# Seven products for eight in the down projection of a decoder trunk's two feed-forward blocks

## The chip, the cores and the metric

One core of a Trainium2 chip runs the whole program. TensorE (PE) multiplies, VectorE (DVE), ScalarE (ACT) and GpSimd (POOL) work on the operands and results, SyncE (SP) issues most DMAs. The metric is the device time of one execution in microseconds (us), the median of several runs.

## The reference

One layer of a hybrid decoder over 1032 tokens (1024 of a prompt, 8 decoded ones), in float32. Its frame is two half-step feed-forward blocks around a mixing block:

```python
def swiglu(x, wg, wu, wd):
    return (jax.nn.silu(x @ wg) * (x @ wu)) @ wd

h = x + 0.5 * swiglu(rmsnorm(x), wg1, wu1, wd1)     # FFN 1
u = rmsnorm(h); z = u @ w_in                        # mixing: attention and mLSTM heads
...
h = h + 0.5 * swiglu(rmsnorm(h), wg2, wu2, wd2)     # FFN 2
h = h + sigmoid(rmsnorm(h) @ w_ple_gate) * ple
```

D_MODEL is 1024, D_FF 2816. The change is in the last product of `swiglu`, the "down" product of 1032 tokens x 2816 by 2816 x 1024, which both FFNs have.

## The kernel before

Activations lie with features on the 128 partitions and tokens along the free axis. Tokens are cut in three groups of N = 344 (`GS`) or four quarters of QN = 258 (`QS`); two quarters are a half (`hf`). D_FF is NF = 22 blocks of 128 features, in NP = 11 pairs. A float32 product is made of three matmuls on operands that are split in an upper part (made by ACT, `hh`, `wh`) and a lower part (made by DVE, `hl`, `wl`); `split` writes both and `mm3` issues upper x upper, upper weight x lower activation, lower weight x upper activation, in this order. So the second matmul of a tile needs the lower part of the activation.

`ffn` does one FFN. Its **gate and up stage** already makes seven products for eight: `chain(i)` multiplies 2 x 2 blocks of weights by sums of 2 x 2 blocks of activations, on 258 tokens at a time, and leaves in the tile `hp` (128 x 4 x 258, per half of the tokens) the product of gate and up for one pair of feature blocks and two quarters. `store` writes it to device memory (`hidd`, a DMA on POOL's queue).

The **down stage** runs in five passes over (half `mh` of the 1024 outputs, group of tokens): `[(0,(0,1)),(0,(2,)),(1,(0,)),(1,(1,)),(1,(2,))]`. A pass has 22 steps, one for each feature block, and a step four blocks of 128 outputs, so that a pass holds 4 (in the first pass 8) of the eight PSUM banks. Weights (`load_wd`, 512 KB for two steps) and `hp` (`load_hid`, 516 KB for three steps) come five steps (`AHEAD_D`) ahead, each through `split`. After a pass the accumulators `pd` are added to the residual `h` on DVE (line 585: h = 0.5 * pd + h; an eviction below), and after the passes of the second output half the norm of that group for the next stage is begun (`nxt.a`: squares on ACT, sums on POOL and DVE; `nxt.b` some microseconds later: a matmul `ns` with ones, lines 276 and 242 to 244, and the multiplies `xf` of line 287).

PE and SP run in the order of the code. The order of ACT, DVE and POOL is set when the program is built, by a scheduler; on the chip each engine then runs its list in this order, and an instruction that waits holds up those behind it.

Of the kernel before, what the change touches and what calls it, by code (L numbers as in the profile page):

```python
# [7 lines left out]
F32 = mybir.dt.float32  # L8
F32R = mybir.dt.float32r
# [6 lines left out]
D = 1024  # L16
# [3 lines left out]
G = 3  # L20
# [7 lines left out]
HC = 2 * QN  # L28
NPAIR = NF // 2
NCH = 2 * NPAIR  # L30
AHEAD_D = 5
HEADS = 8
MH = 4
CH = 128
# [9 lines left out]
POOL_LO = 5  # L44
NBIG = 43
LAT_B = 5.0
LAT_IN = (5.0, 4.0, 12.0)
LAT_P = (5.0, 5.0, 20.0)
AH_IN = {(3, 12): (0,), (4, 4): (1,), (4, 12): (2,)}
PL_A, PL_B = 13, 5  # L50
BUILD_AT = (2, 4, 5, 6)
AH_P = {(3, 12): (0,), (4, 4): (1,), (4, 10): (2,), (4, 16): (3,)}
POOL_FIN = (1, 3, 5)
FIN_ORDER = (0, 1, 2, 4, 3, 6, 5, 7)
PJ = 2
# [84 lines left out]
def trunk(ctx: ExitStack, tc, I, O):  # L140
# [249 lines left out]
    def ffn(build, X, pre, part, resid, h, nxt, ahead, lat, aheads):  # L390

        W = [I["wg" + part], I["wu" + part]]
        wd = I["wd" + part]
        hidd = tc.dram_tile([NF, 128, T], F32, name="hid" + part)
        wraw, ops, gens = pre

        def want(i):
# [22 lines left out]

        gs = [None, None]

        def store(i, hf, o):
            pool.dma_start(out=hidd[i - 1:i + 1, :, hf * HC:(hf + 1) * HC].rearrange("a p c -> p a c"),  # L426
                           in_=o.rearrange("p (a q) n -> p a (q n)", a=2))

        def plain(i, hf):
            o = B([128, 4, QN], F32, "hp" if i % 2 else "gs")  # L430
            for q in range(2):
                for a in range(2):
                    ps = PS([128, QN], "cp")
                    for kh in range(2):
                        mm(ps, ops[i]["p%d" % (2 * a + kh)], X[hf][("b1", "b2")[kh] + "12"[q]], kh == 0, kh == 1)
                    d = o[:, 2 * a + q]
                    if i % 2 == 0:
                        act.activation(d, ps, AF.Silu)
                    else:
                        dve.tensor_tensor(out=d, in0=ps, in1=gs[hf][:, 2 * a + q], op=ALU.mult)  # L440
                yield
            if i % 2 == 0:
                gs[hf] = o
            else:
                gs[hf] = None
                X[hf].pop("b12")
                store(i, hf, o)
            if hf == 1:
                ops.pop(i)

        def chain(i):
# [4 lines left out]
            def product(ps, n, first, lst):  # L456
                for hf in range(2):
                    mm(ps[hf], ops[i][n], X[hf][n], first, lst)
                    yield hf
                ops[i].pop(n)  # L460
                if last:
                    for hf in range(2):
                        X[hf].pop(n)
                    fetch(("b11", "b21", "t2", "t1", "t3", "t4").index(n) - 1 if n != "b22" else AHEAD_D)

            for hf in range(2):
                b1[hf] = PS([128, QN], "c1")
# [34 lines left out]
            for hf in product(b3, "b22", False, True):  # L502
                dve.tensor_tensor(out=o[hf][:, 1], in0=b3[hf], in1=u2[hf], op=ALU.add)
                b3[hf] = u2[hf] = None
                if not up:
                    act.activation(o[hf][:, 1], o[hf][:, 1], AF.Silu)
                    gs[hf] = o[hf]
                else:
                    for a, b in ((0, 2), (3, 4)):
                        dve.tensor_tensor(out=o[hf][:, a:b], in0=o[hf][:, a:b], in1=gs[hf][:, a:b], op=ALU.mult)  # L510
                    gs[hf] = None
                    store(i, hf, o[hf])
                o[hf] = None
            ops.pop(i)
            ready(i + 1)
            want(i + 2)


        passes = [(0, (0, 1)), (0, (2,)), (1, (0,)), (1, (1,)), (1, (2,))]
        seq = [(p, f) for p in range(len(passes)) for f in range(NF)]  # L520
        wdh, hid = {}, {}

        def load_wd(mh, p):
            raw = B([128, 2, 512], F32, "wr")
            sp.dma_start(out=raw, in_=wd[2 * p:2 * p + 2, :, mh * 512:(mh + 1) * 512].rearrange("f p c -> p f c"))
            hi, lo = (B([128, 2, 512], F32R, x) for x in ("wh", "wl"))
            split(hi, lo, raw)
            wdh[mh, p] = (hi, lo)

        def load_hid(p, g, t):  # L530
            n = min(3, NF - 3 * t)
            raw = B([128, 3, N], F32, "hr")
            sp.dma_start(out=raw[:, 0:n], in_=hidd[3 * t:3 * t + n, :, GS[g]].rearrange("f p c -> p f c"))
            hi, lo = (B([128, 3, N], F32R, x) for x in ("hh", "hl"))
            split(hi[:, 0:n], lo[:, 0:n], raw[:, 0:n])
            hid[p, g, t] = (hi, lo)
# [6 lines left out]
        for n, (p, f) in enumerate(seq):  # L543
            mh, gset = passes[p]
            if f % 2 == 0 and (p == 0 or passes[p - 1][0] != mh):
                loads.append((n, lambda mh=mh, f=f: load_wd(mh, f // 2)))
            if f % 3 == 0:
                for g in gset:
                    loads.append((n, lambda p=p, g=g, f=f: load_hid(p, g, f // 3)))
            if p in (0, 2) and f % 2 == 1 and 10 < f < 18:  # L550
                loads.append((n + AHEAD_D, lambda m=4 * (p // 2) + (f - 11) // 2: load_h(m)))
        def fetch(n):
            while loads and loads[0][0] <= n:
                loads.pop(0)[1]()


        ready(0)
# [11 lines left out]
        for i in range(2, NCH):  # L569
            chain(i)  # L570

        for n, (p, f) in enumerate(seq):
            mh, gset = passes[p]
            fetch(n + AHEAD_D)
            if f == 0:
                acc = {(m, g): PS([128, N], "pd") for m in range(4) for g in gset}
            whi, wlo = wdh[mh, f // 2]
            for m in range(4):
                c = slice(m * 128, (m + 1) * 128)
                for g in gset:  # L580
                    hi, lo = hid[p, g, f // 3]
                    mm3(acc[m, g], whi[:, f % 2, c], wlo[:, f % 2, c], hi[:, f % 3, :], lo[:, f % 3, :], f == 0, f == NF - 1)
                    if f == NF - 1:
                        t = h[4 * mh + m][:, GS[g]]
                        dve.scalar_tensor_tensor(out=t, in0=acc.pop((m, g)), scalar=0.5, in1=t, op0=ALU.mult, op1=ALU.add)
            whi = wlo = hi = lo = None
            if f % 2 == 1 and gset[-1] == G - 1:
                wdh.pop((mh, f // 2))
            if f % 3 == 2 or f == NF - 1:
                for g in gset:  # L590
                    hid.pop((p, g, f // 3))
            em.spend(1.9 * len(gset))
            for i in aheads.get((p, f), ()):
                ahead(i)
            if f == NF - 1 and mh == 1:
                g = gset[0]
                nxt.a(g)
                em.later(lat[g], lambda g=g: nxt.b(g))


    ones = C([128, 128], name="ones")
# [1094 lines left out]
def _layout(x):  # L1696
# [11 lines left out]
    for i in "12":  # L1708
        a["wg" + i] = tiles(f[f"w_ff{i}_gate"][0])
        a["wu" + i] = tiles(f[f"w_ff{i}_up"][0])  # L1710
        a["wd" + i] = np.ascontiguousarray(f[f"w_ff{i}_down"][0].reshape(NF, 128, D))
    kr = QL + KV
    mq = kr + 32
    mi = mq + 2048
# [89 lines left out]
```

## Time and profile before

| | us |
|---|---|
| median of 3 runs (lowest, highest) | 2272.29 (2268.96, 2274.8) |
| the profiled execution: its time, its span | 2269.88, 2268.1 |
| PE busy | 2204.2 (97%) |
| DVE busy | 1260.9 (56%) |
| ACT busy | 896.9 (40%) |
| POOL busy | 351.4 (15%) |
| first to last start of a `pd` matmul, FFN 1 | 502.9 to 769.2 |
| the same, FFN 2 | 1890.3 to 2157.7 |

The span is what the profiler saw from first to last instruction; 1.78 us of the execution lie around it. PE's idle share is 3%, spread over the program. In the views a row gives the start, the duration, engine, line, operation and the names of output and inputs; what stands in square brackets is the idle time ahead of it and what ended that.

### The profile page before, as it was taken

How to read it: one execution, taken by the hardware profiler on the slowest of the kernel's cores; microseconds unless marked ns; L12 is line 12 of the kernel's file. 1: busy time of each engine (PE TensorE's matmuls, PEld its weight loads, DVE VectorE, ACT ScalarE, POOL GpSimd, SP SyncE). 2: the span in 40 equal slices, each digit the busy share in tenths (PEclk: the TensorE clock that was granted, in tenths of full speed). 3: DMA queues.
4: the chain of work that ended last, by engine and by line, in shares of the span. 5: the costliest groups of instructions: out<-in, count | busy, mean ns of one | idle time of the engine just before them, and what ended most of it. 6: DMA issues, size and time to landing. Idle time of an engine off the chain costs nothing. (4 is left out here: it accounts for less than half of the span.)

```text
span 2268.1 us, 38221 instructions
## 1 busy us (share of the span) xinstructions
PE 2204.2 (97%) x15697; PEld 2095.2 (92%) x15697; DVE 1260.9 (56%) x2365; ACT 896.9 (40%) x1736; POOL 351.4 (15%) x363
## 2 busy tenths in 40 slices
PE   8999999999999999999999999999999999999897
PEld 7999999999998999999955569999999999999897
DVE  6755555453345446546666777765554555334555
ACT  6333333342323323444465653433333334233353
POOL 2000000000002121111177514100000000001123
PEclk8999999999999999999999999999999999999998
DMA  6122212254543521323455531322122217362413
GB/s 243 38 75 94 75 59 96 72 185 148 175 140 87 176 45 48 116 76 98 155 159 142 161 119 36 115 79 81 57 94 75 93 67 247 117 198 77 128 52 109
DMA packets 115767, 249.91 MB, mean 110 GB/s; under 512 B 12336, under 2 KB 64144, under 8 KB 115592
## 3 DMA queue, kind: packets, MB, share of 16 engines
q1 hardware_dynamic: 96664, 193.42, 26.7%
q0 software_dynamic: 15472, 49.82, 6.5%
q10 hardware_dynamic: 3456, 4.23, 0.6%
q8 instruction: 123, 2.02, 0.4%
q14 instruction: 52, 0.43, 0.1%
HBM read 196.29 MB, written 51.13 MB: 109 GB/s over the span
## 5 line engine op out<-in xcount | busy, mean ns | idle before, releaser
L418 PE MATMUL c<-xh,wh 128*128 128x258 f32 x1920 | 543.3, 283 | 0.0
L419 PE MATMUL c<-xl,wh 128*128 128x258 f32 x1920 | 542.3, 282 | 0.0
L420 PE MATMUL c<-xh,wl 128*128 128x258 f32 x1920 | 542.1, 282 | 0.0
L419 PEld LDWEIGHTS c<-xl,wh 128*128 128x128 f32 x1920 | 363.7, 189 | 0.0
L420 PEld LDWEIGHTS c<-xh,wl 128*128 128x128 f32 x1920 | 362.6, 189 | 0.0
L418 PEld LDWEIGHTS c<-xh,wh 128*128 128x128 f32 x1920 | 362.4, 189 | 0.0
L190 DVE TENSOR_TENSOR wl<-wr,wh 128x1024 fp32r<-128x1024 f32 x210 | 259.6, 1239 | 174.8 <-ACT wh L186 121.1
L205 PE MATMUL pd<-hl,wh 128*128 128x344 f32 x1056 | 342.2, 324 | 12.7 <-DVE hl L190 12.7
L204 PE MATMUL pd<-hh,wh 128*128 128x344 f32 x1056 | 342.5, 324 | 7.7 <-ACT hh L186 7.7
L206 PE MATMUL pd<-hh,wl 128*128 128x344 f32 x1056 | 340.8, 323 | 0.0
L186 ACT CAST wh<-wr 128x1024 fp32r<-128x1024 f32 x210 | 219.1, 1049 | 173.1 <-DMA wr<-in_wd 86.1
L205 PEld LDWEIGHTS pd<-hl,wh 128*128 128x128 f32 x1056 | 201.4, 191 | 15.8 <-DVE hl L190 15.4
L204 PEld LDWEIGHTS pd<-hh,wh 128*128 128x128 f32 x1056 | 201.5, 191 | 9.8 <-ACT hh L186 9.4
L206 PEld LDWEIGHTS pd<-hh,wl 128*128 128x128 f32 x1056 | 201.4, 191 | 0.0
L204 PE MATMUL pz<-u,wh 128*128 128x344 f32 x528 | 172.0, 326 | 0.0
L205 PE MATMUL pz<-u,wh 128*128 128x344 f32 x528 | 169.0, 320 | 1.1 <-DVE u L190 0.8
L206 PE MATMUL pz<-u,wl 128*128 128x344 f32 x528 | 168.7, 319 | 0.0
L426 POOL DMA_DIRECT2D hid<-hp x44 | 31.4, 714 | 885.1 <-DVE hp L510 779.8
L190 DVE TENSOR_TENSOR hl<-hr,hh 128x1032 fp32r<-128x1032 f32 (+1 forms) x96 | 109.3, 1157 | 99.2 <-ACT hh L186 98.8
L262 POOL TENSOR_TENSOR sq<-sq,sq 128x344 f32<-128x344 f32 (+1 forms) x62 | 69.3, 1118 | 555.2 <-ACT sq L257 542.9
L186 ACT CAST hh<-hr 128x1032 fp32r<-128x1032 f32 (+1 forms) x96 | 92.8, 982 | 154.2 <-DMA hr<-hid 143.3
L205 PEld LDWEIGHTS pz<-u,wh 128*128 128x128 f32 x528 | 99.4, 188 | 2.3 <-DVE u L190 1.5
(397 smaller groups left out, 4250.6 us busy)
## 6 DMA issues: line engine op xcount, KB each, us to landing
hr<-hid SPq DMA_DIRECT2D x84, 516.0 KB, 4.3
hid<-hp POOLq DMA_DIRECT2D x44, 516.0 KB, 4.3
wr<-in_wg SPq DMA_DIRECT2D x44, 512.0 KB, 4.4
wr<-in_wu SPq DMA_DIRECT2D x44, 512.0 KB, 4.0
wr<-in_wd SPq DMA_DIRECT2D x44, 512.0 KB, 5.2
wr<-in_w_in SPq DMA_DIRECT2D x22, 512.0 KB, 3.8
h<-hsp SPq DMA_DIRECT2D x16, 516.0 KB, 4.2
xr<-in_xT SPq DMA_DIRECT2D x8, 516.0 KB, 9.7
```

Of the source, the lines that this page charges most:

```text
L186: act.copy(hi, src)
L190: dve.tensor_tensor(out=lo, in0=src, in1=hi.bitcast(F32), op=ALU.subtract)
L204: pe.matmul(ps, whi, xhi, start=first, stop=False)
L205: pe.matmul(ps, whi, xlo, start=False, stop=False)
L206: pe.matmul(ps, wlo, xhi, start=False, stop=last)
L262: pool.tensor_tensor(out=acc[0], in0=acc[0], in1=q, op=ALU.add)
L418: pe.matmul(ps, whi[:, c], xhi[:, k, :], start=first and k == 0, stop=False, skip_group_check=True)
L419: pe.matmul(ps, whi[:, c], xlo[:, k, :], start=False, stop=False, skip_group_check=True)
L420: pe.matmul(ps, wlo[:, c], xhi[:, k, :], start=False, stop=last and k == 3, skip_group_check=True)
L426: pool.dma_start(out=hidd[i - 1:i + 1, :, hf * HC:(hf + 1) * HC].rearrange("a p c -> p a c"), in_=o.rearrange("p (a q) n -> p a (q n)", a=2))
```

## The change

The down product is made with seven products for eight too. The four blocks of weights are (half of the features, half of the outputs), each 1408 x 512. The tokens are cut in two halves of two quarters. Table `DOWN` has for each of the seven products the one or two weight blocks and their sign, the number of the activation operand for each token half, and the one or two blocks of the result (output half, quarter, sign) to which it is added.

- The activation operands are four blocks or sums of blocks, ready in device memory: `store` makes five sums of 128 x 258 on DVE at the end of each up chain and half, and sends seven operands with two DMAs on POOL's queue where there was one.
- The down stage is 7 products x 2 token halves x 11 steps of 12 matmuls on 258 tokens: 1848 matmuls of 258 columns for 1584 of 344. The 11 steps of one product and half are called a chunk here; there are 14 chunks, with 13 boundaries, in an FFN.
- `load_w` loads one or two blocks of weights (two in five of the seven products) and adds them on DVE (128 x 1024) ahead of `split`; `load_x` loads an operand four steps at a time. Loads are issued by the step numbers `W_ISSUE` and `X_LEAD` (8 steps ahead). The eight tiles of the residual `h` are loaded at the stage's start.
- An accumulator holds 128 x 258 and is added to one or two places of `h`. After a chunk stand 8 evictions (4 where a product has one target), 96 in an FFN where there were 24. The norm of groups 0 and 1 begins after the last product's first half, that of group 2 after its second.

```diff
-        hidd = tc.dram_tile([NF, 128, T], F32, name="hid" + part)
+        hidd = tc.dram_tile([7, 2, 128, NP, QN], F32, name="hid" + part)
...
+        def store(i, hf, o, n):
+            p = i // 2
+            b11, b12, b21, b22 = (o[:, j] for j in ((0, 1, 2, 3), (1, 0, 3, 2))[hf])
+            dve.tensor_tensor(out=n[:, 0], in0=b11, in1=b22, op=ALU.add)
+            dve.tensor_tensor(out=n[:, 1], in0=b11, in1=b12, op=ALU.add)
+            dve.tensor_tensor(out=n[:, 2], in0=b21, in1=b22, op=ALU.add)
+            dve.tensor_tensor(out=b12, in0=b12, in1=b22, op=ALU.subtract)
+            dve.tensor_tensor(out=b21, in0=b21, in1=b11, op=ALU.subtract)
+            pool.dma_start(out=hidd[0:4, hf, :, p, :].rearrange("a p c -> p a c"), in_=o)
+            pool.dma_start(out=hidd[4:7, hf, :, p, :].rearrange("a p c -> p a c"), in_=n[:, 0:3])
...
+        def load_w(i, c):
+            (b1, b2, sign), n = DOWN[i][0], min(2, NP - 2 * c)
...
+            if b2 is not None:
+                r2 = B([128, 2, 512], F32, "wr")
+                sp.dma_start(out=r2[:, 0:n].rearrange("p k f -> p (k f)"), in_=wd[b2, :, cc])
+                dve.tensor_tensor(out=raw[:, 0:n], in0=raw[:, 0:n], in1=r2[:, 0:n], op=ALU.add if sign > 0 else ALU.subtract)
             hi, lo = (B([128, 2, 512], F32R, x) for x in ("wh", "wl"))
...
+        for n in range(NSTEP):
+            fetch(n)
+            i, hf, p = n // (2 * NP), n // NP % 2, n % NP
+            if p == 0:
+                acc = [PS([128, QN], "pd") for _ in range(4)]
...
+                mm3(acc[m], whi[:, p % 2, c], wlo[:, p % 2, c], xhi[:, p % 4, :], xlo[:, p % 4, :], p == 0, p == NP - 1)
...
+            if p == NP - 1:
+                for m in range(4):
+                    for r, j, sign in DOWN[i][2]:
+                        t = h[4 * r + m][:, QS[j if hf == 0 else 3 - j]]
+                        dve.scalar_tensor_tensor(out=t, in0=acc[m], scalar=0.5 * sign, in1=t, op0=ALU.mult, op1=ALU.add)
...
+            if i == 6 and p == NP - 1:
+                for g in ((0, 1), (2,))[hf]:
+                    nxt.a(g)
+                    em.later(lat[g], lambda g=g: nxt.b(g))
```

The instructions move as follows. First DVE's order at the end of a pass. Before, at the end of the first pass of FFN 1 (`hl_746` is the lower part of the first activation tile of the second pass, `h<-pd` are the evictions of the first pass):

```order
L190 TENSOR_TENSOR hl_746_6153<-hr_744_6150,hh_745_6152 128x1032
L585 SCALAR_TENSOR_TENSOR h_701_5920<-pd_672_5606,h_701_5920 128x344
L585 SCALAR_TENSOR_TENSOR h_701_5920<-pd_673_5607,h_701_5920 128x344
L190 TENSOR_TENSOR hl_749_6231<-hr_747_6228,hh_748_6230 128x1032
L585 SCALAR_TENSOR_TENSOR h_711_5988<-pd_674_5608,h_711_5988 128x344
L585 SCALAR_TENSOR_TENSOR h_711_5988<-pd_675_5609,h_711_5988 128x344
```

After, at the end of the first product's second token half in FFN 1 (`hl_717` is the lower part of the first activation tile of the second product, `wl_714` that of a weight sum for its third and fourth step):

```order
L552 TENSOR_TENSOR wr_711_5974<-wr_711_5974,wr_712_5976 128x1024
L619 SCALAR_TENSOR_TENSOR h_672_5738<-pd_707_5946,h_672_5738 128x258
L619 SCALAR_TENSOR_TENSOR h_686_5786<-pd_707_5946,h_686_5786 128x258
L619 SCALAR_TENSOR_TENSOR h_673_5740<-pd_708_5947,h_673_5740 128x258
L619 SCALAR_TENSOR_TENSOR h_690_5806<-pd_708_5947,h_690_5806 128x258
L619 SCALAR_TENSOR_TENSOR h_677_5748<-pd_709_5948,h_677_5748 128x258
L619 SCALAR_TENSOR_TENSOR h_691_5820<-pd_709_5948,h_691_5820 128x258
L619 SCALAR_TENSOR_TENSOR h_682_5766<-pd_710_5949,h_682_5766 128x258
L619 SCALAR_TENSOR_TENSOR h_696_5843<-pd_710_5949,h_696_5843 128x258
L205 TENSOR_TENSOR wl_714_5980<-wr_711_5974,wh_713_5979 128x1024
L205 TENSOR_TENSOR hl_717_5998<-hr_715_5995,hh_716_5997 128x1032
```

The lower part that stood ahead of the evictions before now stands behind all eight of them and behind a weight's lower part. On PE, at the same place after, the second matmul of the new product reads `hl_717` and the eight evictions read `pd_707` to `pd_710`:

```order
L219 MATMUL pd_710_5949<-hh_705_5942,wh_684_5782 128x258
L220 MATMUL pd_710_5949<-hl_706_5943,wh_684_5782 128x258
L221 MATMUL pd_710_5949<-hh_705_5942,wl_685_5783 128x258
L219 MATMUL pd_732_6135<-hh_716_5997,wh_694_5839 128x258
L220 MATMUL pd_732_6135<-hl_717_5998,wh_694_5839 128x258
```

The last sum of the old product and the first of the new one stand next to each other there, with one matmul between that and the reader of `hl_717`. The third place is DVE's order at the end of the last up chain of FFN 1, after (`hl_662` is the lower part of the first activation tile of the down stage, lines 444 to 448 are the sums of `store`, line 526 the last addition of a chain and line 533 its product with the gate; the tiles `hp_639` and `gs_617` are of the first token half, `hp_641` and `gs_619` of the second):

```order
L526 TENSOR_TENSOR hp_641_5511<-c3_648_5571,u2_646_5568 128x258
L444 TENSOR_TENSOR gs_617_5274<-hp_639_5496 128x258
L445 TENSOR_TENSOR gs_617_5274<-hp_639_5496 128x258
L448 TENSOR_TENSOR hp_639_5496<-hp_639_5496 128x258
L533 TENSOR_TENSOR hp_641_5511<-hp_641_5511,gs_619_5289 128x516
L205 TENSOR_TENSOR hl_662_5673<-hr_660_5670,hh_661_5672 128x1032
L447 TENSOR_TENSOR hp_639_5496<-hp_639_5496 128x258
L444 TENSOR_TENSOR gs_619_5289<-hp_641_5511 128x258
```

Three of the new sums stand between the last addition of the chain and the first operand of the down stage.

## Rows read from the trace of the kernel before

**Rows 1.** Busy time by stretch: start and end, us, engines, PEclk, DMA share, GB/s.

```profile
284.00:340.00 56.00, 56.00 (x468) 56.00 (x468) 31.40 (x50) 19.86 (x37) 1.43 (x2) 1.00 0.18 59
502.90:769.50 266.60, 256.09 (x1592) 253.44 (x1591) 120.00 (x131) 83.39 (x107) 26.81 (x24) 0.98 0.45 146
567.00:624.00 57.00, 57.00 (x364) 57.00 (x363) 19.69 (x21) 19.83 (x22) 3.66 (x3) 1.00 0.57 175
1890.30:2158.00 267.70, 257.83 (x1592) 255.29 (x1591) 120.14 (x132) 84.35 (x108) 26.86 (x24) 0.97 0.45 145
```

**Rows 2.** DVE's timeline at the end of the first pass, FFN 1.

```profile
582.89 0.98 DVE L585 SCALAR_TENSOR_TENSOR h<-pd,h 128x344 f32<-128x344 f32 x2 [6.42 <-PE pd L206]
583.79 1.22 DVE L190 TENSOR_TENSOR hl<-hr,hh 128x1032 fp32r<-128x1032 f32 x1
584.93 2.62 DVE L585 SCALAR_TENSOR_TENSOR h<-pd,h 128x344 f32<-128x344 f32 x6
```

**Rows 3.** DVE's timeline at the end of the third pass, FFN 1.

```profile
667.86 0.98 DVE L585 SCALAR_TENSOR_TENSOR h<-pd,h 128x344 f32<-128x344 f32 x2 [10.88 <-PE pd L206]
668.77 1.22 DVE L190 TENSOR_TENSOR hl<-hr,hh 128x1032 fp32r<-128x1032 f32 x1
```

**Rows 4.** PE's timeline at the same place.

```profile
670.04 0.43 PE L205 MATMUL pd<-hl,wh 128*128 128x344 f32 x1 [0.64 <-DVE hl L190]
```

**Rows 5.** DVE's groups of instructions by form: count, busy us, mean ns.

```profile
L190 DVE TENSOR_TENSOR wl<-wr,wh 128x1024 fp32r<-128x1024 f32 x210 | 259.6, 1239 | 174.8 <-ACT wh L186 121.1 <-PE c L420 27.2 <-PE pd L205 15.8
...
L510 DVE TENSOR_TENSOR hp<-hp,gs 128x516 f32<-128x516 f32 x40 | 27.8, 696 | 1.4
...
L337 DVE TENSOR_TENSOR xf<-xf,xf 128x1032 f32<-128x1032 f32 x16 | 20.6, 1286 | 0.3
...
L490 DVE TENSOR_TENSOR hp<-c,u 128x258 f32<-128x258 f32 x40 | 16.9, 423 | 16.8 <-ACT u L489 16.8
```

**Rows 6.** PE's timeline in the fourth and fifth pass, FFN 1: matmuls after a wait.

```profile
688.40 0.43 PE L204 MATMUL pd<-hh,wh 128*128 128x344 f32 x1 [0.66 <-ACT hh L186]
...
691.16 0.42 PE L205 MATMUL pd<-hl,wh 128*128 128x344 f32 x1 [2.33 <-DVE hl L190]
...
718.97 0.42 PE L204 MATMUL pd<-hh,wh 128*128 128x344 f32 x1 [1.00 <-ACT hh L186]
...
720.24 0.43 PE L205 MATMUL pd<-hl,wh 128*128 128x344 f32 x1 [0.84 <-DVE hl L190]
...
740.50 0.65 PE L204 MATMUL pd<-hh,wh 128*128 128x344 f32 x1 [2.57 <-ACT hh L186]
...
743.24 0.65 PE L205 MATMUL pd<-hl,wh 128*128 128x344 f32 x1 [2.09 <-DVE hl L190]
```

**Rows 7.** Busy time by stretch around these waits (columns as in the first group).

```profile
692.20:695.60 3.40, 3.40 (x14) 3.40 (x13) 1.28 (x2) 0.24 (x1) 0.00 (x0) 0.50 0.00 0
717.00:722.00 5.00, 3.15 (x19) 2.63 (x18) 3.32 (x7) 3.13 (x6) 1.52 (x1) 1.00 0.43 121
740.00:746.80 6.80, 4.21 (x13) 3.85 (x14) 5.46 (x5) 2.45 (x3) 1.59 (x2) 0.50 0.13 47
```

**Rows 8.** DVE's timeline at the end of the gate and up stage, FFN 1.

```profile
503.06 0.43 DVE L503 TENSOR_TENSOR hp<-c,u 128x258 f32<-128x258 f32 x1 [0.24 <-PE c L420]
```

**Rows 9.** DMA issues of 502 to 770: count, KB each, median us to landing.

```profile
hr<-hid SPq DMA_DIRECT2D x34, 516.0 KB, 3.8
...
hid<-hp POOLq DMA_DIRECT2D x2, 516.0 KB, 8.5
```

**Rows 10.** GB/s of the core in 40 slices of 0 to 60.

```profile
GB/s 0 209 322 372 371 368 391 385 400 409 415 418 396 396 406 413 398 407 414 160 215 151 0 0 0 0 5 297 372 328 61 11 0 0 298 197 205 0 0 0
```

**Rows 11.** DVE's timeline at a norm's multiplier, FFN 1.

```profile
677.03 0.52 DVE L276 TENSOR_SCALAR v<-ns 128x344 f32<-128x344 f32 x1 [2.01 <-ACT r L275]
```

**Rows 12.** The page's part 5: gate and up matmuls, POOL's DMA issues.

```profile
L418 PE MATMUL c<-xh,wh 128*128 128x258 f32 x1920 | 543.3, 283 | 0.0
...
L426 POOL DMA_DIRECT2D hid<-hp x44 | 31.4, 714 | 885.1 <-DVE hp L510 779.8
```

More of the change, by code (lines that the diff above doesn't have):

```diff
@@ L30 @@
 NCH = 2 * NPAIR
-AHEAD_D = 5
+NP = NF // 2
+NWC = (NP + 1) // 2
+NXC = (NP + 3) // 4
+W_ISSUE = (-17, -13, -9, -5, -2, 2)
+X_LEAD = 8
+H_AT = -2
+DOWN = (((0, None, 0), (1, 0), ((0, 1, 1), (1, 1, 1))),
[6 rows of a table added]
+NSTEP = 7 * 2 * NP
 HEADS = 8
@@ L444, in plain @@
             else:
+                X[hf].pop("b12")
+                store(i, hf, o, gs[hf])
                 gs[hf] = None
-                X[hf].pop("b12")
-                store(i, hf, o)
             if hf == 1:
@@ L510, in chain @@
                         dve.tensor_tensor(out=o[hf][:, a:b], in0=o[hf][:, a:b], in1=gs[hf][:, a:b], op=ALU.mult)
+                    store(i, hf, o[hf], gs[hf])
                     gs[hf] = None
-                    store(i, hf, o[hf])
                 o[hf] = None
@@ L542, in ffn @@
         loads = []
[L543 to L551, printed above, removed]
+        for i in range(7):
+            n = 2 * NP * i
+            for c in range(NWC):
+                loads.append((n + W_ISSUE[c], len(loads), lambda i=i, c=c: load_w(i, c)))
+            for hf in range(2):
+                for t in range(NXC):
+                    loads.append((n + NP * hf + 4 * t - X_LEAD, len(loads), lambda i=i, hf=hf, t=t: load_x(i, hf, t)))
+        for m in range(KD):
+            loads.append((H_AT + m, len(loads), lambda m=m: load_h(m)))
+        loads.sort(key=lambda x: x[0:2])
         def fetch(n):
             while loads and loads[0][0] <= n:
-                loads.pop(0)[1]()
+                loads.pop(0)[2]()
         ready(0)
@@ L570, in ffn @@
             chain(i)
[L572 to L577, printed above, removed]
+        for n in range(NSTEP):
[3 more added lines that the diff above has]
+                acc = [PS([128, QN], "pd") for _ in range(4)]
+            (whi, wlo), (xhi, xlo) = wdh[i, p // 2], xh[i, hf, p // 4]
@@ L586, in ffn @@
[L586 to L598, printed above, removed]
+                mm3(acc[m], whi[:, p % 2, c], wlo[:, p % 2, c], xhi[:, p % 4, :], xlo[:, p % 4, :], p == 0, p == NP - 1)
@@ new lines, in ffn @@
+            whi = wlo = xhi = xlo = None
+            if hf == 1 and (p % 2 == 1 or p == NP - 1):
+                wdh.pop((i, p // 2))
+            if p % 4 == 3 or p == NP - 1:
+                xh.pop((i, hf, p // 4))
+            if p == NP - 1:
[3 more added lines that the diff above has]
+                        dve.scalar_tensor_tensor(out=t, in0=acc[m], scalar=0.5 * sign, in1=t, op0=ALU.mult, op1=ALU.add)
+                acc = None
@@ L601, in trunk @@
+            em.spend(1.44)
+            for j in aheads.get(n, ()):
+                ahead(j)
+            if i == 6 and p == NP - 1:
+                for g in ((0, 1), (2,))[hf]:
+                    nxt.a(g)
+                    em.later(lat[g], lambda g=g: nxt.b(g))
     ones = C([128, 128], name="ones")
```

46 lines of the change are left out of this document (18 added, 28 removed), and 6 rows, old and new, of the table DOWN.

## The prediction

> **What bounds the kernel now.** I read the busy time by stretch first [rows 1]. From 567 to 624 us, inside the first pass of FFN 1's down stage, PE is busy for all of 57.00 us and starts 364 matmuls of 344 columns: 57.00/364 = 0.1566 us each, at the full clock (PEclk 1.00). From 284 to 340 us, in the gate and up stage, 468 matmuls of 258 columns take 56.00 us: 0.1197 each. So PE is the bound, and the time goes by columns. But the down stages of 1584 matmuls would take 1584 x 0.1566 = 248.0 us, and take 266.6 and 267.7. The 18.6 and 19.7 that are over are waits at the ends of passes and slow clock after them, and there I looked next, in DVE's and PE's timelines.
>
> At the end of a pass DVE has two things to do: empty the accumulators, and make the lower part of the next pass's first activations, which PE's second matmul needs. At 583.79 the `hl` that stands among the evictions is already that of a later tile (front's order: `hl_746`, which PE needs first, stands ahead of all evictions), and PE has no wait there [rows 1, 2]. At 667.86 two evictions come first, the `hl` PE needs begins at 668.77 and takes 1.22, and PE starts at 670.04, after a wait of 0.64 [rows 3, 4]. DVE ran exactly in its built order at both places, so the order of after tells what will wait.
>
> **The change part by part.**
>
> PE's own work: 1848 matmuls x 0.1197 = 221.1 us per FFN, 442.3 in both. Both stages of before take 266.6 + 267.7 = 534.3. If nothing waited, 92.0 us would be gained.
>
> Boundaries: this is where I put most weight. In after's order, at most of the 13 boundaries in each FFN the lower part for the next chunk stands behind the evictions of the one that ends. I count from the first matmul of the chunk's last step. That step is 12 x 0.1197 = 1.44 us, and the next chunk's second matmul is due at 1.44 + 0.12 = 1.56. The first accumulator is complete after three matmuls, the last of which ends at 2 x 0.12 + 0.28 [rows 12]; I take 0.55. Evictions of 344 columns follow each other every 2.62/6 = 0.44 us [rows 2], which is a duration of 0.515 less an overlap of some 0.07; an operation of 258 columns lasts 0.423 [rows 5], so I take 0.36 apart. Eight end their turn at 0.55 + 8 x 0.36 = 3.43. A weight's lower part follows in ten cases: 1.15 (583.79 to 584.93 for the like of it, [rows 2]). Then `hl`, 1.22, and 0.05 to PE's start (668.77 + 1.22 to 670.04, [rows 3, 4]): 3.43 + 1.15 + 1.22 + 0.05 = 5.85, and PE waits 5.85 - 1.56 = 4.3. Without the weight it waits 3.1. The order has, in both FFNs together, 10 boundaries with eight evictions and a weight (43 us), 7 with eight evictions alone (21.7), and 9 with four evictions or with some of them behind `hl`, between 1.0 and 2.2 each by the same steps (15.4). The sum is 80.1. The bounds are 0.64 a boundary, the wait at 670.04 (26 x 0.64 = 17), and 5 (130), if DVE comes to the boundaries late: its work in a product of two weight blocks and two targets is 6 additions of 1.29, 6 x 1.24 and 6 x 1.25 of lower parts and 16 x 0.36 of evictions, some 28 us, beside 31.6 of PE [rows 5], so it need not. I take 80.
>
> Start of the stage: DVE's last addition of the chain starts at 503.06, 0.16 after PE's first matmul of the down stage at 502.9 [rows 1, 8]. Behind it the order has three sums of 258 columns and the multiply of 516 (0.65 with its overlap, [rows 5]) ahead of `hl_662`: 0.16 + 0.36 + 3 x 0.36 + 0.65 + 1.22 + 0.05 = 3.5, against 0.12: a wait of 3.4, twice 6.8. The activations of steps 9 to 11 need the last store. That is issued some 3 us after the gate and up stage, needs 8.5 us to land and 3.8 to be read back [rows 9], and 2.3 for both parts: near 17.5, where PE comes to 3.4 + 8 x 1.44 = 15. Two us each, 4 in both. Bounds 0 and 10.
>
> End of the stage: the second activation tile of the last chunk (`hl_992`) stands on DVE behind the squares' sums of two groups and the multiplier of a norm, which at the like place of before is at 677.03, some 6 us after the evictions [rows 3, 11]. With `hl` it comes some 10 to 12 us after the chunk's start, and PE is there after 4 steps, 5.8. I take 6 in FFN 1, where a weight's lower part stands in between too, 4 in FFN 2, and 1.5 each for the first product of the stage behind: 13. Bounds 5 and 25.
>
> In the gate and up stage, 5 sums x 2 halves x 11 pairs = 110 x 0.42 = 46 us of DVE's time per FFN. I cost them at nothing: DVE is busy for 31.40 of 56 us there, PE waits for none of its products, and POOL's 44 more DMA issues of 0.71 fall where it is busy for 1.43 of 56 [rows 1, 12]. Without that cover they would be 92 us.
>
> DMA: the down stage moves 12 weight blocks of 2.88 MB, 14 operands of 1.45 and 4.2 of residual, 59 MB in some 260 us, or 227 GB/s, where before it moved 146; the core reaches 300 to 418 at its start [rows 1, 10]. Not the bound, so nothing.
>
> Without the clock: 442.3 + 80.1 + 6.8 + 4 + 13 = 546.2, which is 11.9 over 534.3.
>
> The clock: after waits of 0.66 and 2.33 at 688.40 and 691.16, and of 2.57 and 2.09 at 740.50 and 743.24, the granted clock is 0.50 from 692.2 to 695.6 and from 740.0 to 746.8, the lower of the clock's two levels (1.2 and 2.4 GHz), while 1.00 and 0.84 at 718.97 and 720.24 leave it at 1.00 [rows 6, 7]. A spell of 3.4 to 6.8 us costs half of itself, 1.7 to 3.4; I take 2.5. The waits of 4.3, at the start and at the end are as long as those that brought it on (14 spells), those of 3.1 lie between, and I take half of the 7. 17.5 x 2.5 = 44. Bounds 0 and 26 x 3.4 = 88.
>
> Sum 546.2 + 44 = 590; profiled execution 2269.9 + 590 - 534.3 = 2325.6. That execution is 2.4 below the median of the runs shown, which is inside their scatter. Forecast **2326**.
>
> **The rivals.**
>
> *The evictions are hidden (faster).* A chunk takes four of the eight banks, the next one the other four, so PE needn't wait for any eviction: only the place of one `hl` makes it wait. If the engines are so far ahead that the boundaries cost as little as at 582.89, near nothing, the result is 2269.9 - 534.3 + 442.3 + 6.8 + 4 + 13 + 10 for some leftover = 2212. It decides below some 2.5 us a boundary with the clock kept: (92.0 - 23.8)/26 = 2.6. For it stands the end of the first pass, against it 670.04, where two evictions ahead were enough for a wait [rows 2 to 4], and the eight in after's order. The Trainium skill, Perfetto Trace Analysis, "Matmuls" under "Optimizing Tensor Performance", speaks for this rival: groups of matmuls that rotate through different banks let the evacuation of one overlap the matmuls of the next. By that rule the time would be 2212; the trace agrees at 582.89 and not at 670.04, since the engine that evacuates also makes the next operand.
>
> *The waits come, the clock holds.* 2269.9 + 11.9 = 2282. For it the waits of 718.97, which left the clock alone; against it that those of 740.50 are shorter than 4.3 and did not.
>
> *The loads are late too.* A read behind the store and two weight blocks for one: 2 us more at each boundary with its clock, 26 x 2.2 = 57, 2382. Against it 8 steps of lead, 11.5 us, for a landing of 3.8 [rows 9].
>
> *The sums come to light in the gate and up stage*: up to 92 more, 2418.
>
> **How the numbers follow.** Likeliest case 0.66, own range 2300 to 2360; clock held 0.17 (2275 to 2300); hidden 0.08; late loads 0.07; sums 0.02. The range reaches from the clock-held case to the bounds of the boundaries' wait: 2276 to 2370. A difference of 0.3% (7 us) is about what a measurement of this kernel can tell from no change. Faster is the hidden case, 0.08; the same needs a clock that is held and boundaries at some 4 us less in all, 0.05; slower 0.87.
>
> **What would show it.** At the boundaries PE's second matmul of a chunk should wait some 3 to 4.3 us with DVE's `hl` as its releaser, in 17 of 26 places, and the clock stand at 0.50 after most. Matmuls between should keep 0.1197. The first product of the stage should wait 3.4, the last chunk 4 to 6, and no `c` matmul in the gate and up stage should wait for DVE. The prediction is wrong if the `hl` rows come ahead of the evictions in time, if the waits are there and PEclk stays at 1.00, or if the releasers are DMAs.

## The result, and the profile after

The changed kernel takes 2359.8 us in the median (2357.35 to 2362.66), the kernel before 2270.97 beside it: a ratio of 1.039, 95% interval [1.037, 1.0409]. The forecast was 2326, with a range of 2276 to 2370.

The page's first part for the changed kernel (span 2357.1, against 2268.1):

```profile
PE 2194.3 (93%) x16225; PEld 2077.4 (88%) x16225; DVE 1464.2 (62%) x2817; ACT 912.6 (39%) x1764; POOL 387.1 (16%) x407
```

PE is busy 10 us less than before, and the span is 89 longer: PE waits. Where, the first and last starts of the down products tell (the tile view of `pd`, FFN 1 and FFN 2):

```profile
L219 PE MATMUL pd<-hh,wh x616: 276/283/583, 506.8 to 800.3; 128*128 128x258 f32 x154
...
L221 PE MATMUL pd<-hh,wl x616: 276/283/421, 510.5 to 800.5; 128*128 128x258 f32 x154
...
L219 PE MATMUL pd<-hh,wh x616: 276/283/547, 1933.9 to 2223.2; 128*128 128x258 f32 x154
...
L221 PE MATMUL pd<-hh,wl x616: 277/283/420, 1937.5 to 2223.5; 128*128 128x258 f32 x154
```

With the starts of the kernel before in the table ahead of the prediction, the 89.0 us come from five stretches:

| stretch | before | after | more |
|---|---|---|---|
| start to the first down product | 502.9 | 506.8 | 3.9 |
| down stage of FFN 1 | 266.3 | 293.7 | 27.4 |
| from there to the first down product of FFN 2 | 1121.1 | 1133.4 | 12.3 |
| down stage of FFN 2 | 267.4 | 289.6 | 22.2 |
| from there to the end of the span | 110.4 | 133.6 | 23.2 |

The down stages, in the view of waits of PE (waited for: us in total, times, longest; first FFN 1, then FFN 2):

```profile
PE pd L220 <- DVE hl L205: 42.3, 17, 3.9
PE pd L219 <- ACT hh L201: 4.9, 3, 2.9
...
PE pd L220 <- DVE hl L205: 42.2, 16, 3.9
PE pd L219 <- ACT hh L201: 1.2, 2, 0.9
```

The releaser is DVE's lower part of the activations, and no DMA (behind the start of the stage a late load stands one step further back, see the third tile below). One of the boundaries, that whose order is shown ahead of the prediction; DVE's timeline:

```profile
548.57 2.76 DVE L619 SCALAR_TENSOR_TENSOR h<-pd,h 128x258 f32<-128x258 f32 x8 [5.07 <-PE pd L221]
551.24 1.21 DVE L205 TENSOR_TENSOR wl<-wr,wh 128x1024 fp32r<-128x1024 f32 x1
552.38 1.22 DVE L205 TENSOR_TENSOR hl<-hr,hh 128x1032 fp32r<-128x1032 f32 x1
```

ACT's timeline just ahead of it:

```profile
543.58 1.05 ACT L201 CAST wh<-wr 128x1024 fp32r<-128x1024 f32 x1 [2.60 <-issue]
544.53 1.05 ACT L201 CAST hh<-hr 128x1032 fp32r<-128x1032 f32 x1
```

And PE's:

```profile
549.46 0.28 PE L219 MATMUL pd<-hh,wh 128*128 128x258 f32 x1
553.65 0.58 PE L220 MATMUL pd<-hl,wh 128*128 128x258 f32 x1 [3.91 <-DVE hl L205]
```

This is what to see: the upper parts were ready at 544.6 and 545.6, DVE had nothing to do for 5.07 us, and it stood before an eviction that PE had not released yet, with the two lower parts behind it in its list. Eight evictions in 2.76, the weight, the activation: PE starts at 553.65 where it could at 549.58. The waits at the 13 boundaries, as the time between the starts around each less one regular spacing of 0.12, are 4.1 (ten times in both FFNs together), 2.9 to 3.0 (seven) and 1.0 to 2.2 (nine): 38.3 in FFN 1 and 38.6 in FFN 2.

The clock, in the busy time by stretch (columns as in [rows 1]: the whole stage of FFN 1, two of the spells in it, one at the start of the mixing block, the stage of FFN 2, one behind it):

```profile
506.80:800.80 294.00, 246.80 (x1855) 242.07 (x1854) 174.74 (x239) 85.25 (x106) 18.27 (x17) 0.92 0.60 204
552.90:559.70 6.80, 6.05 (x28) 6.05 (x29) 5.34 (x5) 2.31 (x3) 0.00 (x0) 0.50 0.64 217
597.30:600.70 3.40, 3.40 (x18) 3.40 (x17) 2.28 (x3) 2.00 (x2) 0.00 (x0) 0.50 0.46 180
812.30:822.50 10.20, 6.72 (x22) 6.28 (x23) 7.39 (x9) 4.13 (x7) 2.13 (x2) 0.50 0.42 145
1933.90:2223.80 289.90, 246.40 (x1856) 241.87 (x1855) 174.34 (x237) 86.35 (x107) 18.34 (x17) 0.92 0.61 208
2263.00:2276.70 13.70, 5.26 (x17) 4.82 (x18) 9.93 (x13) 6.93 (x12) 6.54 (x6) 0.50 0.13 39
```

PEclk is 0.92 over each down stage, where it was 0.98 and 0.97 [rows 1]: 47.8 and 44.4 us of them at the lower level (1.2 GHz).

Behind the stages PE waits again (waits of PE from 801 to 830, then from 2224 to 2275):

```profile
PE pz L219 <- ACT wh L201: 6.2, 1, 6.2
PE pz L221 <- DVE wl L205: 1.3, 1, 1.3
...
PE pl L219 <- ACT wh L201: 15.0, 2, 11.5
PE pl L221 <- DVE wl L205: 3.4, 3, 2.3
```

Here it is weights, not activations. ACT's timeline around the longest of them:

```profile
2257.80 0.55 ACT L290 ACTIVATE r<-ns,epsc 128x344 f32<-128x344 f32 x1
2261.14 1.45 ACT L201 CAST xp<-xf 128x344 fp32r<-128x344 f32 x3 [2.80 <-DVE xf L302]
...
2267.85 0.48 ACT L201 CAST xp<-xf 128x344 fp32r<-128x344 f32 x1 [0.67 <-DVE xf L302]
...
2269.99 1.04 ACT L201 CAST wh<-wr 128x1024 fp32r<-128x1024 f32 x1
```

The upper part of a weight for a product of the first token group stands behind the casts of the third group's norm, and each of these waits for a multiply on DVE. PE has nothing to do from 2259.6 to 2271.1, with 13.7 us of slow clock around it.

### The profile page after: what moved, and what is told of

It reads as the page before. It is cut to its first block, busy times and chain, and to the rows that moved or that the text cites. A ratio compares the mean times of both kernels' runs of the same rounds, so it can differ in the third digit from the quotient of the medians.

```text
span 2357.1 us, 40138 instructions
## 1 busy us (share of the span) xinstructions
PE 2194.3 (93%) x16225; PEld 2077.4 (88%) x16225; DVE 1464.2 (62%) x2817; ACT 912.6 (39%) x1764; POOL 387.1 (16%) x407
## 4 chain that ended last, share of the span: by engine, by line
PE 71%; DVE 12%; issue 9%; DMA 4%; ACT 2%; POOL 1%; SPq 0%; DVEq 0%; ACTq 0%; POOLq 0%
PE c L434 8%; PE c L436 8%; PE c L435 8%; PE pd L220 6%; PE pd L221 5%; PE pd L219 5%; PE pz L221 3%; PE pz L219 3%; PE pz L220 3%; PE pss L1413 2%; DVE h L619 2%; DMA wr<-in_wd 2%; DVE hl L205 2%; DVE xf L302 1%; DVE wl L205 1%
## 5 line engine op out<-in xcount | busy, mean ns | idle before, releaser
L220 PE MATMUL pd<-hl,wh 128*128 128x258 f32 x1232 | 370.0, 300 | 84.5 <-DVE hl L205 84.5
L201 ACT CAST wh<-wr 128x1024 fp32r<-128x1024 f32 x250 | 255.2, 1024 | 392.5 <-DVE wr L552 188.2
L205 DVE TENSOR_TENSOR wl<-wr,wh 128x1024 fp32r<-128x1024 f32 x250 | 303.2, 1214 | 137.8 <-ACT wh L201 104.6
L219 PE MATMUL pd<-hh,wh 128*128 128x258 f32 x1232 | 366.3, 297 | 6.2 <-ACT hh L201 6.1
L221 PE MATMUL pd<-hh,wl 128*128 128x258 f32 x1232 | 365.4, 297 | 0.0
L220 PEld LDWEIGHTS pd<-hl,wh 128*128 128x128 f32 x1232 | 251.4, 204 | 91.9 <-DVE hl L205 91.7
L219 PEld LDWEIGHTS pd<-hh,wh 128*128 128x128 f32 x1232 | 251.2, 204 | 8.1 <-ACT hh L201 7.8
L221 PEld LDWEIGHTS pd<-hh,wl 128*128 128x128 f32 x1232 | 251.6, 204 | 0.0
L450 POOL DMA_DIRECT2D hid<-gs x44 | 33.1, 751 | 839.9 <-DVE gs L445 700.2
L619 DVE SCALAR_TENSOR_TENSOR h<-pd,h 128x258 f32<-128x258 f32 x192 | 68.1, 419 | 155.1 <-PE pd L221 154.0
```

Source lines behind the costliest of these rows:

```text
L201: act.copy(hi, src)
L205: dve.tensor_tensor(out=lo, in0=src, in1=hi.bitcast(F32), op=ALU.subtract)
L219: pe.matmul(ps, whi, xhi, start=first, stop=False)
L220: pe.matmul(ps, whi, xlo, start=False, stop=False)
L221: pe.matmul(ps, wlo, xhi, start=False, stop=last)
L450: pool.dma_start(out=hidd[4:7, hf, :, p, :].rearrange("a p c -> p a c"), in_=n[:, 0:3])
```

## The experiments

Down stage: from the first to the last start of its products; entry: from the last down product of FFN 1 to the last product of the mixing block's input projection; tail: from the last down product of FFN 2 to the end. hl_first, fill_waits, one_block and norm_early ran on a chip on which the core of the mixing block takes 71 to 76 us longer in their traces than in that of the changed kernel, and the kernel before takes 2343.24; so kernels are compared by the ratio to the kernel before of the same chip, and by these stretches, which leave that block out.

| kernel | ratio to before | down 1 | entry | down 2 | tail |
|---|---|---|---|---|---|
| before | 1 | 266.3 | 289.7 | 267.4 | 110.4 |
| changed | 1.039 [1.037, 1.0409] | 293.7 | 298.8 | 289.6 | 133.6 |
| hl_first | 0.9987 [0.9971, 1.0003] | 243.0 | 302.4 | 241.6 | 137.1 |
| fill_waits | 1.0245 [1.0222, 1.0269] | 277.0 | 298.8 | 276.9 | 132.3 |
| one_block | 1.0305 [1.0283, 1.0328] | 285.7 | 297.1 | 281.3 | 133.6 |
| norm_early | 1.0323 [1.0299, 1.0346] | 294.5 | 287.8 | 294.9 | 125.2 |
| norm2_later | 1.0382 [1.0365, 1.04] | 293.7 | 307.5 | 290.0 | 125.1 |
| start_first | 1.0409 [1.0392, 1.0427] | 293.7 | 301.7 | 294.1 | 133.7 |
| no_sums | 1.0311 [1.0289, 1.0334] | 290.7 | 297.0 | 291.2 | 130.1 |
| three_orders | 0.9991 [0.9981, 1.0001] | 244.8 | 312.5 | 246.4 | 124.6 |
| four_orders | 0.9945 [0.9928, 0.9961] | 260.2 | 289.6 | 256.0 | 113.6 |
| norm_sixth | 0.9937 [0.9916, 0.9959] | 255.0 | 289.6 | 257.1 | 113.6 |
| norm_free_slot | 0.9866 [0.9842, 0.989] | 249.0 | 289.7 | 248.2 | 113.7 |
| norm_behind_tile | 0.9879 [0.9863, 0.9896] | 247.9 | 289.8 | 247.1 | 113.9 |

**hl_first: the order at the boundaries.** `low` keeps the instruction that makes each lower part; `issue_after` queues what is traced in its block behind it on the same engine, and makes it wait for nothing.

```diff
+                ahd = [low["x", i + hf, 1 - hf, 0]] if n < NSTEP - 1 else []
+                with ExitStack() as st:
+                    for x in ahd:
+                        st.enter_context(tc.issue_after(x.ins))
-                for m in range(4):
+                    for m in range(4):
...
```

> The evictions of each chunk are queued on DVE behind the lower part of the next chunk's first activation tile; nothing else is changed. Theory (the place of that lower part makes the wait): its input is ready some 3 us before the first eviction could start (upper part done at 545.6, eviction at 548.6 in the changed kernel), so the 77 us of waits at the 26 boundaries all but vanish, and the slow clock behind them with them (17 boundaries of 3 us or more, about 35 us): 2360 - 77 - 35 = 2248, at most 2265. Rival (DVE has too much to do in the down stage): the waits come back at the later tiles of the chunk and the time stays above 2310.

The down stages are 23 and 26 us shorter than before the change, and 99 us in all shorter than in the changed kernel. DVE's timeline at the same boundary:

```profile
543.46 1.23 DVE L204 TENSOR_TENSOR hl<-hr,hh 128x1032 fp32r<-128x1032 f32 x1
544.86 2.76 DVE L624 SCALAR_TENSOR_TENSOR h<-pd,h 128x258 f32<-128x258 f32 x8 [0.17 <-PE pd L220]
```

PE's waits in the stage of FFN 1:

```profile
PE pd L219 <- DVE hl L204: 10.2, 12, 3.2
PE pd L218 <- ACT hh L201: 1.2, 1, 1.2
...
```

The same evictions take the same 2.76, and PE runs through the boundary, as it does at 25 of the 26; the first one of FFN 2 keeps a wait of 1.65. What else is left in the stage of FFN 1 is the 3.2 of its start, 0.7 at the second tile of most chunks, and some 3 each at the second tile of the second and of the last chunk. PEclk over the stage is 0.98. The ratio fell by 4.0%, some 92 us; 112 were expected. Entry and tail grew by 3.6 and 3.5, since their late weights are waited for longer when PE comes sooner. The theory holds for the boundaries; by the rival, a DVE that has too much to do, no more than 50 of the 112 would have come back. A rule of the Trainium skill belongs here (Perfetto Trace Analysis, "Matmuls" under "Optimizing Tensor Performance": matmul groups that take turns between banks let one be emptied under the next one's matmuls). In this kernel it holds in hl_first and not in the changed kernel, where the same banks take turns and PE waits 4.1 us.

**fill_waits: the price of the clock alone.** `FILL` has 22 matmuls for the boundaries with a wait of 3.0, 32 for those with 4.1.

```diff
+            if p == 0:
+                for _ in range(FILL[part][n // NP]):
+                    pe.matmul(acc[0], whi[:, 0, 0:128], xhi[:, 0, :], start=True, stop=True)
             for m in range(4):
```

> At the 17 boundaries with a wait of 3 us or more PE makes 22 or 32 more matmuls (2.6 and 3.8 us of them, on an accumulator that is then begun anew) in the place of most of the wait; nothing else is changed. Theory (a wait of 3 to 4 us brings the slow clock): the 17 spells of 3.4 to 6.8 us at half clock at these places disappear and give back some 34 us: 2326. Rival (the slow clock comes from something else, or the forecast's 2.5 us a spell was really waiting time): no change, 2355 to 2365; if the added matmuls themselves cost, more than 2365.

The ratio fell by 0.0145, 33 us. The busy time by stretch of its two down stages:

```profile
505.90:783.20 277.30, 261.50 (x2104) 256.74 (x2103) 174.88 (x240) 85.33 (x106) 18.26 (x17) 0.98 0.63 216
1989.20:2266.40 277.20, 261.76 (x2082) 257.82 (x2081) 175.56 (x240) 86.39 (x107) 18.31 (x17) 0.97 0.63 217
```

There are 248 and 226 matmuls more, and the stages are 16.7 and 12.7 us shorter. PEclk is back at 0.98 and 0.97, with 27.3 us at the lower level in both stages for 92.2. So the slow clock follows the waits, and its price is near the forecast's.

**one_block: DVE's load and the DMAs.**

```diff
             if b2 is not None:
-                r2 = B([128, 2, 512], F32, "wr")
-                sp.dma_start(out=r2[:, 0:n].rearrange("p k f -> p (k f)"), in_=wd[b2, :, cc])
-                dve.tensor_tensor(out=raw[:, 0:n], in0=raw[:, 0:n], in1=r2[:, 0:n], op=ALU.add if sign > 0 else ALU.subtract)
+                pass
```

> The second weight block of the five products that have two is neither loaded nor added, so that the weights differ: 60 loads of 512 KB and 60 DVE additions of 1.2 us less, in both FFNs together. Theory (the boundary waits come from the order, not from the load on DVE or the DMAs): the waits keep their places behind the evictions, some with one lower part of weights more or less ahead; 2335 to 2360. Rival (DVE or the DMAs are overloaded in the down stage): with 72 us less of DVE's work and 31 MB less the time falls below 2310.

DVE lost 32 us of work in a stage (142.37 busy for 174.74) and the stage 8; the ratio came down by 0.0085, 19 us. PE's waits in FFN 1's stage stay:

```profile
PE pd L220 <- DVE hl L205: 35.2, 16, 3.2
PE pd L219 <- ACT hh L201: 4.2, 2, 2.9
```

Neither DVE's load nor the loads' bytes make the waits at the boundaries. Those of 4.1 are 2.95 there, where the weight's lower part comes behind `hl` on DVE.

**norm_early, norm2_later: the stages behind.** The norm of token group 1, whose tokens no product behind the fifth touches, begins after the sixth product's first half; or the norm of group 2 is issued later (`LAT` has for each group the us from `nxt.a` to `nxt.b`).

```diff
-            if i == 6 and p == NP - 1:
-                for g in ((0, 1), (2,))[hf]:
+            if p == NP - 1:
+                for g in {(5, 0): (1,), (6, 0): (0,), (6, 1): (2,)}.get((i, hf), ()):
```

```diff
-LAT_IN = (5.0, 10.0, 8.0)
-LAT_P = (5.0, 10.0, 15.0)
+LAT_IN = (5.0, 10.0, 20.0)
+LAT_P = (5.0, 10.0, 28.0)
```

> The norm of token group 1 is begun after the first half of the sixth product (its tokens are complete by then), not with group 0's after the last product's first half. Theory (the stages behind the down stages start late because three norms fall into the last 16 us): the waits of 6.5 and 1.8 us at the first products of the mixing block and of 11.8 and 0.9 after FFN 2, with their slow clock (10.2 and 13.7 us at half speed), go away: 2360 - 8 - 5 - 12 - 7 = 2328. Rival (the end's work is too much for DVE, ACT and POOL wherever it stands): the waits move into the down stage or to groups 0 and 2 and the time stays within 8 us of 2360.

> The changed kernel with the normalisation of token group 2 issued later: 20 in place of 8 us after the first FFN's end, 28 in place of 15 us after the second's. Theory (in the stage after FFN 2 the upper parts of the last weights stand behind seven casts of group 2's norm on ACT, and PE waits 11.5 us for one of them): that wait, the 0.9 behind it and its 13.7 us of slow clock go, some 19 us in the tail, from 117 us between the last down product and the last product of the program to near 98; in the first FFN the 6.2 us stay, since there the weight stands behind group 1's casts: ratio to the kernel before 1.031. Rival (DVE, ACT and POOL are late whatever the order): the wait moves to group 2's own products and the tail keeps 112 to 120 us.

Each cured one end. With group 1's norm early, the entry has no wait and is 11 us shorter, 2 less than before the change; the tail, 8 shorter by the smaller waits ahead of it, kept one of 11.7 for a weight's upper part, so that the wait that I had put down to group 1 was group 2's there. With group 2's norm later that one is gone (tail 8.5 shorter, where a wait of 5.6 for the last norm's sums on POOL came in its place), but the entry is 8.7 longer, since 20 us are too late there. Of 32 and 18 us expected they gave 15 and 2 (from the ratios). The cause is confirmed, a late norm ahead of weights in ACT's list, and the remedy differs by stage.

**start_first.** What DVE does for the last chain is queued behind the down stage's first lower part (the sums of `store` included).

```diff
             for hf in product(b3, "b22", False, True):
-                dve.tensor_tensor(out=o[hf][:, 1], in0=b3[hf], in1=u2[hf], op=ALU.add)
...
+                with ExitStack() as st:
+                    if last:
+                        st.enter_context(tc.issue_after(low["x", 0, 0, 0].ins))
+                    dve.tensor_tensor(out=o[hf][:, 1], in0=b3[hf], in1=u2[hf], op=ALU.add)
...
```

> The changed kernel with the last additions of the last up chain, their products with the gate and the sums of the last store queued on DVE behind the lower part of the down stage's first activation tile (ready on ACT's side at 503.6 us, PE needs it at 506.9). Theory: the wait of 3.3 us at the start of each down stage goes, and with it the slow clock at the start of the second, 8 us in both; the last store comes 1 us later, which may give 1 us back at the third tile: ratio 1.035 to 1.036. Rival (the wait is hidden by another one behind it): less than 3 us, ratio 1.038 to 1.039.

The wait at the first product is gone, and nothing is gained: PE's waits from 504 to 550 there are

```profile
PE pd L219 <- DVE hl L204: 5.8, 4, 2.2
PE pd L218 <- ACT hh L201: 2.6, 1, 2.6
```

and in the changed kernel, from 506 to 550,

```profile
PE pd L220 <- DVE hl L205: 5.8, 4, 3.2
PE pd L219 <- ACT hh L201: 2.0, 2, 1.4
```

The wait goes to the second tile, behind the same work on DVE, and to the third, whose load waits for the last store, which now comes later. The rival was right: the start costs 3.3 only in name.

**no_sums.** The five additions of `store` are left out; the operands sent are other values.

> The changed kernel without the five sums of store (the seven operands are sent with what stands in the two tiles, so that the down products multiply other values; loads, splits and matmuls are the same). Theory (46 us of DVE's time per FFN are hidden in the gate and up stage): the time to the first down product falls by no more than the 4 us by which it rose, and the start's wait of 3.3 us loses the three sums ahead of it, 1.1 us each: 3 to 8 us in all, ratio 1.0355 to 1.038. Rival (the sums cost DVE's time there or through the operands): 20 us or more, ratio below 1.031.

The time to the first down product falls by 3.7, to 503.1, near the 502.9 of the kernel before. One trace of each says that only roughly: in the changed kernel and the eight others here that are the same up to there it lies between 505.0 and 507.3, so the sums account for 2.0 to 4.2. From the gate and up stage's start to the first down product of FFN 2 it falls by 1.9. The rest of the 13 us by which this profiled span is shorter lies in small pieces of other stretches (the down stage of FFN 2 is 1.6 longer), and the ratio fell by 18 us: more than the theory's 8, at the edge of the rival's 20. So the sums are not free; what they cost beside these 4 to 6 us and some 1 us at the start of each down stage was not found. PE's timeline at the start of FFN 1 shows a part of the 3.9; in the changed kernel the first pair's sums stand on DVE there among the lower parts `xl`:

```profile
83.31 0.38 PE L434 MATMUL cp<-xh,wh 128*128 128x258 f32 x1 [0.59 <-ACT xh L201]
84.79 0.39 PE L435 MATMUL cp<-xl,wh 128*128 128x258 f32 x1 [1.10 <-DVE xl L205]
```

and in the kernel before:

```profile
83.08 0.39 PE L419 MATMUL cp<-xl,wh 128*128 128x258 f32 x1 [0.73 <-DVE xl L190]
```

**three_orders, four_orders, norm_sixth: together.** three_orders has the edits of hl_first, start_first and norm2_later; four_orders has norm_early's too, and 12 us for group 2 in FFN 1; norm_sixth is four_orders without the start's edit.

> The evictions behind the next chunk's first lower part, the last chain's work behind the first lower part of the down stage, and group 2's norm later, all three together. If the three costs are separate they add: down stages of 242 - 3 = 239 us each, tail of 98, ratio 0.999 - 0.003 - 0.008 = 0.987 to 0.989. If one only uncovers another: 0.995 to 0.999.

> The same with the norm of group 1 begun after the first half of the sixth product, and group 2's norm 12 us after the end in the first FFN. If group 1's casts are what stands ahead of the third weight at the start of the mixing block (9.2 us there with the evictions moved), 8 to 12 us less than with three: ratio 0.983. If the earlier norm only moves DVE's work into the down stage: no less than with three.

> The same as the four orders (norm of group 1 after the sixth product's first half) without the change at the start of the stage. The start's edit gave nothing by itself, so the same time as the four orders within 4 us: ratio 0.993 to 0.996.

Three gave no more than hl_first alone (0.9991): the entry of 312.5 ate what the tail gave. The fourth brought the entry back to that before the change and the tail to within 3.3 us of it, but its down stages are 15 and 10 us longer than with three. Without the start's edit the time is the same (0.9937), as start_first lets one expect. PE's timeline in four_orders at the last product's first and second tile:

```profile
722.23 0.58 PE L219 MATMUL pd<-hh,wh 128*128 128x258 f32 x1 [3.18 <-ACT hh L202]
...
736.03 0.58 PE L220 MATMUL pd<-hl,wh 128*128 128x258 f32 x1 [3.08 <-DVE hl L205]
```

There the early norm's multiplies (4.00 us from 714.98 on) stand on DVE ahead of the sums of the last product's weights.

**norm_free_slot, norm_behind_tile.** The sixth product has single weight blocks, so while its operands are in use DVE is least busy; the norm of group 1 goes to its beginning, `(4, 1): (1,)` in the table above and 3 us for `LAT`; hl_first's order and the later norm of group 2 stay. In norm_behind_tile its multiplies are also queued behind that chunk's third lower part.

> Evictions behind the next chunk's first lower part, as before; norm of group 1 begun after the second half of the fifth product, 3 us to its multiplier, so that it falls in the chunks in which the sixth product's single weight blocks are made (no additions on DVE); group 2's norm 12 and 28 us after the ends; the start of the stage as in the changed kernel. If the down stages' 260 and 256 us of the four orders are the early norm colliding with the sums of the last product's weights (waits of 3.5 and 1.5 us at the last product's start, 3.5 at its second tile, with their slow clock): down stages of 243 to 248, mixing entry 290 and tail 94 as there: 2260 - 24 = 2236, ratio 0.983 to 0.987. If the place doesn't matter: 0.994.

> The kernel with the norm in the free slot, and group 1's multiplier and multiplies queued on DVE behind the lower part of that chunk's third activation tile, for which PE waited 5.0 and 4.9 us. Its upper part is ready at 687.8, and PE needs the lower part at 692.7. Theory: both waits go, with the slow clock behind them (3.4 and 6.8 us at half speed): 15 us less, 2229, ratio 0.979 to 0.982. Rival (the norm, 4 us later now, holds up something behind it): not below 0.985.

The place was right: 249.0 and 248.2 for the stages, ratio 0.9866, the best kernel here, 1.3% faster than the kernel before and 5% than the change. One wait stood out in it, PE's timeline:

```profile
697.71 0.58 PE L220 MATMUL pd<-hl,wh 128*128 128x258 f32 x1 [4.86 <-DVE hl L205]
```

Behind the tile, the norm holds up the next chunk's first tile instead:

```profile
701.82 0.39 PE L219 MATMUL pd<-hh,wh 128*128 128x258 f32 x1 [3.51 <-ACT hh L202]
703.09 0.58 PE L220 MATMUL pd<-hl,wh 128*128 128x258 f32 x1 [0.88 <-DVE hl L205]
```

and the time is the same within the intervals, as the rival had it. The norm's eight multiplies, 7.34 us on DVE there, have to stand somewhere in a chunk of 16.

## Why the prediction was right, and where its sum was short

The direction and the mechanism were right: the boundaries' lower parts are late by their place in DVE's list, and the clock falls behind them. Term by term, forecast and measured:

- **PE's own work**, 221.1 a stage: FFN 1's stage in hl_first is 243.0, of which some 17 are waits, taken between starts, and some 5 the clock of 0.98, so 221 without them. The spacing between boundaries is the 0.12 of the forecast.
- **Boundaries**, 80.1: measured 76.9, with 4.1 and 2.95 for the forecast's 4.3 and 3.1, ten and seven of them as counted. hl_first shows the cause.
- **Start**, 6.8: measured 3.32 twice, 6.6. But start_first shows that only the place of this wait hangs on the order, not its cost.
- **Third tile at the start**, 4: measured 0.75 in FFN 1 and nothing in FFN 2 there. At the next chunk's second tile there are 2.9 and 1.3 that I had not named; that their sum, 5.0, is near the 4 is luck. The landing that I had in mind is behind these too. ACT's and DVE's parts release PE, but the upper part waits for its load. The load of the third tile waits in SP's list for the landing of the last store, and with it all loads behind it, for 16.8 us; then the DMA engines are full (share 1.00, 384 GB/s).
- **Last chunk**, 6 and 4: measured 5.9 and 3.6. In FFN 1 the larger part is not DVE's list, as I had it, but ACT's: PE idles 2.92 for the tile's upper part and 2.11 for its lower one.
- **Clock**, 44: half of the 47.8 and 44.4 us at the lower level is 46.1, in 22 spells where 17.5 were counted, some of it inside the waits. What the other terms leave of the stages' 583.3 is 43. fill_waits gave 33 us back for the 17 boundaries that it fills.
- **Gate and up stage**, nothing: measured 3.9 and some 2, and no_sums gives both back, as far as the scatter of the start lets one say. The cover held in the chains and not in the first pair, where DVE is also making the operands.
- **The stage behind**, "1.5 each for the first product of the stage behind": this is the step that failed in its size. It measured 9.1 at the entry (298.8 for 289.7) and 23.2 in the tail. I had looked at what DVE does between the last chunk's tiles and priced the first product behind them. The cost is made by ACT's list: the three norms' roots on ACT (`r<-ns`) now start at 784.4, 796.6 and 823.7 in FFN 1, where before they started at 676.4, 726.6 and 785.2, and the casts that follow stand ahead of the next stage's weights; on it comes the slow clock of a wait of 6 to 12 us.

The rows of that late load, in the changed kernel (waits of SP's queue from 500 to 545, ACT's timeline, the busy time from 516 to 545):

```profile
SPq L560 <- DMA hid<-hp: 16.8, 1, 16.8
...
535.30 1.05 ACT L201 CAST hh<-hr 128x1032 fp32r<-128x1032 f32 x1 [0.21 <-DMA hr<-hid]
...
516.00:545.00 29.00, 24.34 (x181) 23.32 (x180) 13.70 (x18) 7.83 (x9) 0.00 (x0) 0.94 1.00 384
```

With fewer loads, in one_block, the two waits at the second tile are 0.5 and nothing. So the forecast's "not the bound, so nothing" for the DMAs held for the stage as a whole (204 GB/s) and not for some 30 us behind its start. No run moved the store or that load, so what another order of the loads would give back stays open.

So the stages themselves were forecast to 587 (without the 3 behind them) and took 583.3, and 2326 fell short of 2359.8 by what lies behind the stages and a little in the gate and up stage: 2359.8 is the very end of my own range of 2300 to 2360. Of the rivals, that of the hidden evictions describes a kernel that exists, hl_first, though with 2268 (0.9987 of 2270.97) and not 2212: its entry and tail are 39 us longer than before the change, and its stages are 485, where that case has 466 and 10 for some leftover. The clock-held case would have given some 46 us less in the stages than was measured; the traces and fill_waits exclude it. Late loads at every boundary are excluded by the releasers and by one_block; late they are only behind the start of each stage, as said.

## What to carry to other kernels

When a change cuts a stage into more pieces, look at the engine that both empties the accumulators and makes the next piece's operands, and read in its built order which stands first: an eviction that waits for PE blocks an operand that has been ready for microseconds, and other banks do not help. Queue the operand ahead by an explicit order edge; it moves no work and was worth 4% here. And price what a change does to the next stage's operands in every engine's list, not only in the one that is busiest: work that was spread over passes and now falls together at the end shows up as a late weight one stage on. The same holds for the queue that issues the loads: one load that waits for a store holds up those behind it, and a mean of GB/s over the stage does not show it.

## What the runs showed of the hardware

In the changed kernel a spell at 1.2 GHz (3.4 to 6.8 us) begins around the end of each of the seventeen boundary waits of 2.9 to 4.1 us; of the nine shorter ones only the longest, 2.2 us, has one. Matmuls whose results are thrown away, put in the place of such a wait, are worth more than they cost: 474 more of them, 29 us shorter stages. And one of the chips ran the mixing block in 452 to 457 us from the last input product to the next gate and up stage, where the others took 377 to 381 for the same instructions, with some 100 us at the slower clock in it for some 20; what makes it wait there was not looked into and stays open.
